# Moving the loads of the cumulative sums to another queue, and one group's stage ahead by a projection, in a hybrid decoder step

## The chip, the cores and the metric

The kernel runs on one core of a Trainium2 chip. The metric is device microseconds of one execution. A core has a matrix engine, TensorE (PE in the profile; PEld is its weight load), three other engines, VectorE (DVE), ScalarE (ACT) and GpSimd (POOL), and SyncE (SP), which here only issues DMAs. Each engine works through its own list of instructions in order and waits on semaphores. [...] The profile writes SPq and ACTq for the issuing of DMAs by SyncE and ScalarE.

## What is computed

Two layers of a hybrid decoder, one step, on a prompt of 256 tokens and on 8 samples of 4 tokens that share the weights: 288 columns in all. Everything is float32.

```python
for l in range(DEPTH):
    x = x + 0.5 * swiglu(rmsnorm(x, norm_ffn1[l]), ...)
    m = mixer(rmsnorm(x, norm_mix[l]), ...)      # gated linear attention and a Mamba-2 branch, merged
    x = x + m
    x = x + 0.5 * swiglu(rmsnorm(x, norm_ffn2[l]), ...)
```

The change lies in the Mamba-2 branch (SSD): 32 heads of 64 channels in 4 groups, 128 state dimensions. For each head, `x` is weighted by `dt`, and with the cumulative sums of the decays and the group's B and C:

```python
acum = cumsum(dt * A)                                        # along the tokens
seg = exp(where(causal, acum[t] - acum[s], -inf))
cb = einsum('nbtgd,nbsgd->nbtsg', Cc, Bc)                    # once per group
y_diag = einsum('nbtsg,nbtsgh,nbsghp->nbtghp', cb, seg, xg)
dS = einsum('nbsgd,nbsgh,nbsghp->nbghpd', Bc, exp(acum[-1] - acum), xg)
y_off = einsum('nbtgd,nbtgh,nbghpd->nbtghp', Cc, exp(acum), h_prev)
```

Outputs are the tokens of both sets and all new states, among them the new SSD states of the prompt (`ssm_p`) and of the samples (`ssm_s`).

## The kernel before

Activations lie with their channels on the partitions, `[128, 288]` a block of 128 channels. A projection makes one such block of output. Its weights come as one DMA of 512 KB into `wr` (`weights`, L179, SyncE's queue, four buffers), ScalarE rounds them into `wh` (L166), VectorE takes the rest into `wl` (L172, three buffers of each), and TensorE adds 24 products in one buffer of `psg` (three): 16 with `wh` (L185, L186) and 8 with `wl` (L188). So each projection needs SyncE, ScalarE, VectorE and TensorE in turn.

In the mixer the Mamba-2 branch is the generator `ssd`. It takes 16 channel blocks j of two heads each; four blocks are a group g. Between its stages it yields a number n, and its caller runs n projections of other parts of the layer there (z, output gates and merge gates), so TensorE has large products beside the small ones. `blocks` makes such projections and hands out their results.

The stages, by line:

- `stage_bc(g)`: projections of the group's B and C, each with its causal convolution (`conv`: ScalarE L874 to L879 copies the projection out of `psg` into `cbuf`, VectorE L881 three times, ScalarE L883, VectorE L885 and L889 give `bcf`).
- `stage_group(g)`: transposes of B into one `pst` buffer; VectorE's L949 reads the last part of it into `bpk`. Products of B and C into a second buffer (L952 to L954), masked into `cb` (L957) and `cbs` (L961). `pst` has four buffers, which all small products share.
- `stage_load(j)`: the samples' states `st`, two DMAs of 256 KB (L989, SyncE; eight buffers). `stage_t(j)`: VectorE transposes them (L998) for TensorE's L1016.
- `stage_x(j)`: the projection and convolution of block j of `x` (`xs`). At its end SyncE issues the load of `acb` (L1031): the cumulative sums of the block's two heads, read from device memory and spread over all 128 partitions, `[128, 512]` words; `acb` has two buffers.
- `stage_m(j)`: ScalarE reads `acb` six times (L1046 to L1048, two heads) into the decay masks `m`, takes their exponential (L1050); VectorE weights `x` (L1054, L1057, L1060, L1063).
- `stage_y(j)`: TensorE's eight products (L1074 to L1081) into one `pst` buffer and the two outer products of the samples' states (L1099), one buffer each; VectorE L1083, L1093 and L1101; ScalarE's copy of the prompt's state into `so` (L1088); the stores of `st` (L1103) and, every second block, of `so` (L1106), all on SyncE.

The loop over j runs `stage_load(j + 3)`, `stage_x(j + 2)`, `stage_m(j + 1)`, yields one projection, then, for j of 2, 6 and 10, runs the next group's `stage_group`, then `stage_y(j)` and further stages.

The order in which the program is written isn't the order on the engines: a scheduler puts each engine's instructions into a list when the program is built. So the change of a few lines moves instructions on all engines, and the order on an engine is shown below as it is built.

## Time and profile before

| | |
|---|---|
| median of 3 runs | 1818.79 us (1818.36 to 1819.49) |
| the profiled execution | 1818.43 us, span 1816.6 us |
| granted clock of TensorE, mean | 0.998 of full speed |
| busy: TensorE / VectorE / ScalarE / GpSimd | 98% / 69% / 57% / 19% |
| bytes moved by DMA | 325.59 MB, 179 GB/s over the span |

Times in the views count from the start of the span. In a timeline the bracket at the end of a line is the time in which the engine stood idle just before the instruction, and what it then waited for last; an x and a number after it join alike instructions in a row. The SSD stage of layer 1 lies at about 369 to 600 us, that of layer 2 at about 1265 to 1500. Since TensorE has 35 us of idle time in all, its own gaps are the place to look, and other engines' waits where such a gap leads to them.

### The profile page before, as it was taken

How to read it: one execution, taken by the hardware profiler on the slowest of the kernel's cores; microseconds unless marked ns; L12 is line 12 of the kernel's file. 1: busy time of each engine (PE TensorE's matmuls, PEld its weight loads, DVE VectorE, ACT ScalarE, POOL GpSimd, SP SyncE). 2: the span in 40 equal slices, each digit the busy share in tenths (PEclk: the TensorE clock that was granted, in tenths of full speed). 3: DMA queues.
4: the chain of work that ended last, by engine and by line, in shares of the span. 5: the costliest groups of instructions: out<-in, count | busy, mean ns of one | idle time of the engine just before them, and what ended most of it. 6: DMA issues, size and time to landing. Idle time of an engine off the chain costs nothing.

```text
span 1816.6 us, 36201 instructions
## 1 busy us (share of the span) xinstructions
PE 1781.6 (98%) x14304; PEld 1722.5 (95%) x14304; DVE 1257.0 (69%) x2091; ACT 1042.3 (57%) x1970; POOL 349.0 (19%) x453
## 2 busy tenths in 40 slices
PE   8999999999999999999999999999998999999997
PEld 8999999889899999999999999998888999999997
DVE  6555578689898767555565556777889987665554
ACT  6444476577677545444454445665877765554443
POOL 1000000055786400000000000000577671000000
PEclk9999999999999999999999999999999999999999
DMA  7655654976878755555555556558778776555553
GB/s 214 172 170 160 164 148 124 276 196 178 216 213 221 197 170 170 167 163 163 170 169 166 166 162 161 147 170 245 195 192 218 210 214 183 170 163 164 169 161 90
DMA packets 613117, 325.59 MB, mean 179 GB/s; under 512 B 17090, under 2 KB 607858, under 8 KB 612948
## 3 DMA queue, kind: packets, MB, share of 16 engines
q1 hardware_dynamic: 612900, 323.15, 63.3%
q8 instruction: 112, 1.84, 0.4%
q14 instruction: 57, 0.47, 0.1%
q10 hardware_dynamic: 48, 0.13, 0.0%
HBM read 293.01 MB, written 30.22 MB: 178 GB/s over the span
## 4 chain that ended last, share of the span: by engine, by line
PE 52%; DVE 3%; ACT 3%; DMA 2%; POOL 1%; issue 1%; DVEq 0%; ACTq 0%; POOLq 0%
PE psg L185 16%; PE psg L188 16%; PE psg L186 16%; DMA wr<-in_w_in_dram 2%; DVE wl L172 1%; POOL st L1005 1%; PE pst L151 1%; ACT wh L166 1%; DVE sT L998 0%; PE pst L1074 0%; PE pst L1099 0%; ACT bm L979 0%; PE pst L810 0%; DVE cacc L881 0%; PE yo L1016 0%
## 5 line engine op out<-in xcount | busy, mean ns | idle before, releaser
L166 ACT ACTIVATE wh<-wr 128x1024 fp32r<-128x1024 f32 (+1 forms) x498 | 518.5, 1042 | 483.2 <-PE psg L186 379.2
L185 PE MATMUL psg<-xh,wh 128*128 128x288 f32 x2704 | 731.9, 298 | 8.9 <-ACT cbuf L875 4.9
L186 PE MATMUL psg<-xl,wh 128*128 128x288 f32 x2704 | 727.7, 296 | 0.1
L172 DVE TENSOR_TENSOR wl<-wr,wh 128x1024 fp32r<-128x1024 f32 (+1 forms) x496 | 595.1, 1201 | 143.4 <-ACT wh L166 141.6
L185 PEld LDWEIGHTS psg<-xh,wh 128*128 128x128 f32 x2704 | 507.4, 188 | 18.6 <-ACT cbuf L875 5.8
L186 PEld LDWEIGHTS psg<-xl,wh 128*128 128x128 f32 x2704 | 507.4, 188 | 3.9 <-issue 0.9
L188 PE MATMUL psg<-xh,wl 128*128 128x288 f32 x2704 | 415.3, 295 | 0.2
L188 PEld LDWEIGHTS psg<-xh,wl 128*128 128x128 f32 x2704 | 375.8, 188 | 2.4 <-issue 0.9
L1005 POOL TENSOR_SCALAR st<-st,decs 128x128 f32<-128x128 f32 x256 | 241.9, 964 | 41.8 <-DVE sT L998 33.9
L185 PE MATMUL psg<-hh,wh 128*128 128x288 f32 x704 | 188.8, 294 | 0.0
L186 PE MATMUL psg<-hl,wh 128*128 128x288 f32 x704 | 188.3, 294 | 0.0
L185 PEld LDWEIGHTS psg<-hh,wh 128*128 128x128 f32 x704 | 132.1, 188 | 0.1
L186 PEld LDWEIGHTS psg<-hl,wh 128*128 128x128 f32 x704 | 132.1, 188 | 0.0
L313 DVE TENSOR_TENSOR t<-t,psg 128x288 f32<-128x288 f32 x88 | 39.9, 454 | 132.8 <-ACT wh L166 119.5
L382 POOL MEMSET cbuf<- 128x3 f32 x4 | 0.3, 108 | 648.2 <-DVE t L333 648.2
L188 PE MATMUL psg<-hh,wl 128*128 128x288 f32 x704 | 108.3, 294 | 0.0
L310 DVE TENSOR_TENSOR t<-psg,rr 128x288 f32<-128x288 f32 x88 | 40.2, 457 | 87.3 <-PE psg L188 87.2
L188 PEld LDWEIGHTS psg<-hh,wl 128*128 128x128 f32 x704 | 98.1, 188 | 0.0
L881 DVE SCALAR_TENSOR_TENSOR cacc<-cbuf,cw,cacc 128x312 f32<-128x312 f32 x144 | 79.0, 548 | 5.4 <-ACT cacc L879 4.9
L185 PE MATMUL psg<-oh,wh 128*128 128x288 f32 x256 | 69.9, 300 | 0.0
L185 PE MATMUL psg<-yh,wh 128*128 128x288 f32 x256 | 69.7, 299 | 0.0
L186 PE MATMUL psg<-ob,wh 128*128 128x288 f32 x256 | 69.1, 295 | 0.0
(317 smaller groups left out, 2234.4 us busy)
## 6 DMA issues: line engine op xcount, KB each, us to landing
wr<-in_w_ffn_gu_dram SPq DMA_DIRECT2D x176, 512.0 KB
wr<-in_w_in_dram SPq DMA_DIRECT2D x160, 512.0 KB
wr<-in_w_ffn_down_dram SPq DMA_DIRECT2D x64, 448.0 KB
wr<-in_w_ffn_down_dram SPq DMA_DIRECT2D x32, 512.0 KB
st<-in_state_ssm_dram SPq DMA_DIRECT2D x64, 256.0 KB
out_dram<-st SPq DMA_DIRECT2D x64, 256.0 KB
wr<-in_w_proj_ssm_dram SPq DMA_DIRECT2D x32, 512.0 KB
gst<-in_state_gla_dram SPq DMA_DIRECT2D x32, 256.0 KB
```

Source lines behind the costliest of these rows:

```text
L151: T.transpose(out, in_, ident[0:k, 0:k])
L166: A.activation(out=h, in_=raw, func=AF.Copy)
L172: V.tensor_tensor(out=lo, in0=raw, in1=h, op=ALU.subtract)
L185: T.matmul(out, lhsT=h[:, k], rhs=xh[k], start=start and k == 0, stop=False)
L186: T.matmul(out, lhsT=h[:, k], rhs=xl[k], start=False, stop=False)
L188: T.matmul(out, lhsT=lo[:, k], rhs=xh[k], start=False, stop=stop and k == n - 1)
L310: V.tensor_tensor(out=t, in0=pg, in1=r, op=ALU.mult)
L313: V.tensor_tensor(out=h, in0=t, in1=pu, op=ALU.mult)
L382: G.memset(cbufs[i][:, 0:3], 0.0)
L881: V.scalar_tensor_tensor(out=acc, in0=buf[:, i:i + NCV], scalar=w[i], in1=acc, op0=ALU.mult, op1=ALU.add)
L1005: G.tensor_scalar(out=st[:, r], in0=st[:, r], scalar1=decs[:, n:n + 1], scalar2=None, op0=ALU.mult)
```

## The change

Three things are edited. The load of `acb` becomes a stage of its own: for blocks 0 and 1 it is issued by SyncE ahead of the first state loads, for block j + 2 by ScalarE in `stage_m(j)`, behind the six reads of the buffer that it fills anew (14 a layer). The store of `so` is issued by ScalarE in place of SyncE (8 a layer). And `stage_group` of the groups 1 to 3 is called ahead of `stage_m(j + 1)` and of the projection behind it, in place of after it. All else is the same; the lines of the functions below the edit have higher numbers in the changed kernel (L1031 becomes L1035, L1046 L1049, L1054 L1059, L1057 L1062, L1060 L1065, L1063 L1068, L1074 L1079, L1076 L1081, L1083 L1088, L1093 L1098, L1099 L1104, L1101 L1106, L1103 L1108).

```diff
@@ -1027,13 +1027,16 @@
                 conv_last(j, buf)
                 x4 = sp_.tile([128, 128], F32, name="b4", tag="b4", bufs=3)
                 pack(A, x4, xs[:, sp])
-                acb = sp_.tile([128, 2, SEQ], F32, name="acb", tag="acb", bufs=2)
-                nc.sync.dma_start(out=acb, in_=acd[2 * j:2 * j + 2].partition_broadcast(128))
-                R["x", j] = xs, x4, acb
+                R["x", j] = xs, x4
+
+            def stage_acb(j, eng):
+
+                R["acb", j] = acb = sp_.tile([128, 2, SEQ], F32, name="acb", tag="acb", bufs=2)
+                eng.dma_start(out=acb, in_=acd[2 * j:2 * j + 2].partition_broadcast(128))
 
             def stage_m(j):
 
-                xs, x4, acb = R.pop(("x", j))
+                (xs, x4), acb = R.pop(("x", j)), R.pop(("acb", j))
                 cb3 = R["g", j // 4][2]
                 p = pst()
                 tr(p[:, 0:128], xs[:, 0:128])
@@ -1046,6 +1049,8 @@
                     A.activation(out=m[:, hh, 0], in_=ab[:, 0:128], func=AF.Relu, scale=-1.0, bias=A0[:, hd:hd + 1])
                     A.activation(out=m[:, hh, 1], in_=ab[:, 128:256], func=AF.Exp, bias=F0[:, hd:hd + 1])
                     A.activation(out=m[:, hh, 2], in_=ab[:, 128:256], func=AF.Relu, scale=-1.0, bias=A1[:, hd:hd + 1])
+                if j + 2 < 16:
+                    stage_acb(j + 2, nc.scalar)
                 m02 = m[:, :, 0:3:2]
                 A.activation(out=m02, in_=m02, func=AF.Exp, scale=-1.0)
                 xg = sp_.tile([128, 3, 128], F32, name="xg", tag="xg", bufs=2)
@@ -1103,10 +1108,12 @@
                     nc.sync.dma_start(out=state_view(ssm_s, j, hf), in_=sts[hf])
                 if j % 2:
                     hg = j // 2
-                    nc.sync.dma_start(out=ssm_p[l, 0, 4 * hg:4 * hg + 4].rearrange("h p d -> (h p) d").rearrange(
+                    nc.scalar.dma_start(out=ssm_p[l, 0, 4 * hg:4 * hg + 4].rearrange("h p d -> (h p) d").rearrange(
                         "(j q) d -> q j d", q=128), in_=so)
 
             stage_bc(0)
+            for j in range(2):
+                stage_acb(j, nc.sync)
             for j in range(3):
                 stage_load(j)
             yield 1
@@ -1132,11 +1139,11 @@
                 if j == 0:
                     stage_bc(1)
                     stage_pack(1)
+                if j in (2, 6, 10):
+                    stage_group(hg // 2 + 1)
                 if j + 1 < 16:
                     stage_m(j + 1)
                 yield 1
-                if j in (2, 6, 10):
-                    stage_group(hg // 2 + 1)
                 stage_y(j)
                 if j + 2 < 16:
                     stage_t(j + 2)
```

SyncE's list at the start of the SSD stage of layer 1, before and then after (a DMA with its destination and source, its shape, and how many in a row):

```order
L179 DMA wr<-in_w_in_dram 128x8x128 x4
L989 DMA st<-in_state_ssm_dram 128x4x128 x6
L1031 DMA acb<-acd 128x512 x2
L989 DMA st<-in_state_ssm_dram 128x4x128 x2
L179 DMA wr<-in_w_in_dram 128x8x128 x2
L1031 DMA acb<-acd 128x512
L179 DMA wr<-in_w_in_dram 128x8x128 x3
L1031 DMA acb<-acd 128x512
L179 DMA wr<-in_w_in_dram 128x8x128 x5
```

```order
L179 DMA wr<-in_w_in_dram 128x8x128 x4
L1035 DMA acb<-acd 128x512 x2
L989 DMA st<-in_state_ssm_dram 128x4x128 x8
L179 DMA wr<-in_w_in_dram 128x8x128 x9
L1108 DMA out_dram<-st 128x4x128 x2
L989 DMA st<-in_state_ssm_dram 128x4x128
L179 DMA wr<-in_w_in_dram 128x8x128
```

The two first broadcasts stand ahead of the state loads, and the later ones no longer stand between the weights.

VectorE's list around block 6 of layer 1, where group 2 is prepared, before and then after (L949, L957 and L961 are the group's; L881 to L889 are a convolution):

```order
L881 SCALAR_TENSOR_TENSOR cacc<-cbuf_2523,cw,cacc 128x312
L1063 SCALAR_TENSOR_TENSOR xpk<-xpk,call,xd 128x128
L172 TENSOR_TENSOR wl<-wr,wh 128x1024
L885 SCALAR_TENSOR_TENSOR xs<-t_6242,cacc 128x256
L889 SCALAR_TENSOR_TENSOR xs<-t_6242,cacc 128x32
L949 SCALAR_TENSOR_TENSOR bpk<-bpk,call,pst 128x128
L957 TENSOR_TENSOR cb_6319<-pst,call 128x2x128
L1083 SCALAR_TENSOR_TENSOR t_6340<-xs,prm,pst 128x288
L1101 TENSOR_TENSOR st<-st,pst 128x512
L961 TENSOR_TENSOR cbs<-pst,call 128x32
```

```order
L949 SCALAR_TENSOR_TENSOR bpk<-bpk,call,pst 128x128
L881 SCALAR_TENSOR_TENSOR cacc<-cbuf_2523,cw,cacc 128x312
L957 TENSOR_TENSOR cb_6266<-pst,call 128x2x128
L881 SCALAR_TENSOR_TENSOR cacc<-cbuf_2523,cw,cacc 128x312
L961 TENSOR_TENSOR cbs<-pst,call 128x32
L1059 TENSOR_TENSOR xg<-pst,dtm 128x384
L885 SCALAR_TENSOR_TENSOR xs<-t_6244,cacc 128x256
L889 SCALAR_TENSOR_TENSOR xs<-t_6244,cacc 128x32
L1062 TENSOR_TENSOR xd<-pst,dec_2515 128x384
L172 TENSOR_TENSOR wl<-wr,wh 128x1024
L1068 SCALAR_TENSOR_TENSOR xpk<-xpk,call,xd 128x128
L1088 SCALAR_TENSOR_TENSOR t_6342<-xs,prm,pst 128x288
```

The group's three instructions move from behind the convolution's last steps to between its first ones, and stand ahead of the same block's L1059 to L1068.

TensorE's list where block 4's `stage_y` meets the projection behind it (layer 1), before and then after (`oh` and `ob` are the parts of the activations of another projection, `xh` and `xl` those of the next):

```order
L186 MATMUL psg<-ob,wh 128x288
L188 MATMUL psg<-oh,wl 128x288 x8
L1074 MATMUL pst<-m,xg 64x256
L185 MATMUL psg<-xh,wh 128x288
L186 MATMUL psg<-xl,wh 128x288
```

```order
L188 MATMUL psg<-oh,wl 128x288 x8
L1081 MATMUL pst<-m,xg 64x128
L1082 MATMUL pst<-mse,xg 128x32
L1083 MATMUL pst<-call,yos 128x32
L1085 MATMUL pst<-bt,xd 128x128
L1086 MATMUL pst<-bt,xd 128x128
L185 MATMUL psg<-xh,wh 128x288
```

Before, one product of `stage_y` stands ahead of that projection's first matmul and the others behind its last; after, all eight stand ahead of it.

## Rows read from the trace of the kernel before

**Rows 1.** The page's first part: engine, busy us, share, instructions.

```profile
PE 1781.6 (98%) x14304; PEld 1722.5 (95%) x14304; DVE 1257.0 (69%) x2091; ACT 1042.3 (57%) x1970; POOL 349.0 (19%) x453
```

**Rows 2.** TensorE's timeline, layer 1: start us, us, what, [idle before <-releaser].

```profile
382.79 0.40 PE L185 MATMUL psg<-xh,wh 128*128 128x288 f32 x1 [1.07 <-DVE yb L488]
...
386.52 0.70 PE L952 MATMUL pst<-bcf 128*128 128x256 f32 x2 [1.50 <-DVE bcf L885]
...
428.48 0.65 PE L1016 MATMUL yo<-sT,cbd 128*32 128x64 f32 x32 [0.87 <-DVE sT L998]
...
468.60 0.40 PE L185 MATMUL psg<-xh,wh 128*128 128x288 f32 x1 [1.97 <-ACT cbuf L875]
...
508.08 0.50 PE L1099 MATMUL pst<-bm,xpk 128*128 128x512 f32 x1 [1.47 <-DVE bpk L949]
```

**Rows 3.** TensorE's timeline, layer 2.

```profile
1279.07 0.40 PE L185 MATMUL psg<-xh,wh 128*128 128x288 f32 x1 [1.51 <-DVE yb L488]
...
1282.32 0.70 PE L952 MATMUL pst<-bcf 128*128 128x256 f32 x2 [1.01 <-DVE bcf L885]
...
1324.27 0.65 PE L1016 MATMUL yo<-sT,cbd 128*32 128x64 f32 x32 [0.78 <-DVE sT L998]
...
1365.25 0.40 PE L185 MATMUL psg<-xh,wh 128*128 128x288 f32 x1 [2.91 <-ACT cbuf L875]
...
1403.26 0.50 PE L1099 MATMUL pst<-bm,xpk 128*128 128x512 f32 x1 [1.54 <-DVE bpk L949]
```

**Rows 4.** Waits of SyncE's queue, 370 to 590 us: total us, times, longest.

```profile
SPq L179 <- DVE wl L172: 74.4, 31, 6.0
SPq L1031 <- ACT m L1048: 21.4, 4, 12.1
```

**Rows 5.** ScalarE's timeline, the rows read.

```profile
379.15 0.40 ACT L1046 ACTIVATE m<-acb,ac 128x128 f32<-128x128 f32 x1 [3.08 <-DMA acb<-acd]
...
383.74 1.06 ACT L166 ACTIVATE wh<-wr 128x1024 fp32r<-128x1024 f32 x1 [0.41 <-DMA wr<-in_w_in_dram]
...
404.97 1.06 ACT L166 ACTIVATE wh<-wr 128x1024 fp32r<-128x1024 f32 x1 [2.81 <-DMA wr<-in_w_in_dram]
...
464.91 1.06 ACT L166 ACTIVATE wh<-wr 128x1024 fp32r<-128x1024 f32 x1 [3.45 <-DMA wr<-in_w_in_dram]
...
1810.70 0.37 ACTq L1245 DMA_DIRECT2D out_dram<-yo  x1
```

**Rows 6.** Stretches: window, us, busy us (instructions) by engine, granted clock, DMA share, GB/s.

```profile
379.00:390.00 11.00, 8.44 (x60) 7.70 (x59) 7.48 (x13) 10.39 (x33) 11.00 (x17) 1.00 1.14 293
394.00:466.00 72.00, 70.84 (x640) 66.68 (x639) 66.21 (x124) 55.05 (x144) 44.02 (x53) 1.00 0.69 186
...
460.00:462.00 2.00, 2.00 (x17) 2.00 (x17) 1.99 (x4) 1.13 (x3) 2.00 (x2) 1.00 0.66 138
...
470.00:472.00 2.00, 2.00 (x11) 2.00 (x10) 2.00 (x4) 0.40 (x3) 0.00 (x0) 0.50 0.51 122
```

The engines stand there in the order PE, PEld, DVE, ACT, POOL.

**Rows 7.** VectorE's timeline, two places.

```profile
427.29 0.52 DVE L1093 SCALAR_TENSOR_TENSOR yb<-yb,prm,yh 128x288 fp32r<-128x288 f32 x1 [0.68 <-ACT yh L1091]
...
507.69 0.33 DVE L949 SCALAR_TENSOR_TENSOR bpk<-bpk,call,pst 128x128 fp32r<-128x128 f32 x1
```

**Rows 8.** SyncE's timeline: issues of DMAs.

```profile
373.44 2.28 SPq L1031 DMA_DIRECT2D acb<-acd  x2
...
376.85 3.26 SPq L179 DMA_DIRECT2D wr<-in_w_in_dram  x2
...
457.98 0.46 SPq L1031 DMA_DIRECT2D acb<-acd  x1
458.91 1.83 SPq L179 DMA_DIRECT2D wr<-in_w_in_dram  x2
```

**Rows 9.** TensorE's timeline, one block's stage_y: first product, first outer product.

```profile
447.61 0.66 PE L1074 MATMUL pst<-m,xg 128*64 128x256 f32 x4
...
449.33 0.72 PE L1099 MATMUL pst<-bm,xpk 128*128 128x512 f32 x2
```

## The prediction, made before the changed kernel ran

> **What bounds the kernel now.** I read the busy shares first: TensorE (PE) is busy 1781.6 us of a span of 1816.6 [rows 1], so everything still to be had is its 35 us of idle time, and every other wait counts only as far as it ends in one of TensorE's gaps. Next comes TensorE's own timeline, for what released it after each gap. In the part that the change touches (state-space stage, about 369 to 600 us in layer 1 and 1265 to 1500 in layer 2) five gaps stand out in each layer. In layer 1 they are 1.07, 1.50, 0.87, 1.97 and 1.47 us [rows 2], in layer 2 1.51, 1.01, 0.78, 2.91 and 1.54 [rows 3]. That is 6.88 and 7.75 us, 14.6 together. A forecast is a statement on these ten gaps, and on new ones.
>
> Then the queues. SyncE (SP) issues in order, so a load that waits for a buffer holds all behind it. Its issue of `acb` (L1031) waits for the last reader of the old `acb`, ScalarE's L1048, four times in layer 1, 21.4 us in all and 12.1 the longest [rows 4]; the next weights stand right behind it in SyncE's order. ScalarE (ACT) then stands 2.81 us for weights at 404.97 [rows 5], and VectorE (DVE) behind it. VectorE is busy 66.2 of the 72 us from 394 to 466 [rows 6] and so has little room to catch up there.
>
> **The change part by part.**
>
> *Group stage one projection earlier.* TensorE's last gap, 1.47 and 1.54 us at L1099 [rows 2, 3], waits for `bpk`: the second outer product needs the fourth `pst` buffer, which still holds the transposes of the next group until VectorE's L949 has read them, and that stands at 507.69 behind the convolution's L885 and L889 [rows 7]. In the new order L949, L957 and L961 are interleaved with L881, a whole projection ahead of L1106 (the old L1101), so the buffer is free long before. The same instructions run on the same engines, and TensorE's transposes and products of the group only change places with weight matmuls. What is late next at that place is VectorE's L1088 (the old L1083), which the eight products of stage_y feed and which TensorE doesn't wait for there. Price: −1.47 −1.54 = **−3.0**. Bounds: −3.0, and 0 if another user of the four buffers is as late.
>
> *First two `acb` ahead of the states.* ScalarE's 3.08 us at L1046 [rows 5] go: these two broadcasts were issued at 373.44 [rows 8] behind six state loads, now ahead of them. But TensorE is in order and needs more than that. Its next gap, at L952, hangs on C's convolution: L885 needs ScalarE's L883, which stands behind an L166 that itself waited 0.41 us for weights at 383.74 [rows 5]. Those weights were issued from 376.85 on [rows 8] behind eight state loads and two broadcasts; the bytes ahead of them are the same in either order, and the DMAs move 293 GB/s in 379 to 390, with a busy share of 1.14 of their engines [rows 6]: there is no room for more. So when `acb` no longer delays ScalarE, the first gap melts into the second and the end of the pair stays where the weights put it. What is new is `acb` 2: ScalarE now issues it as soon as stage_m(0) has read `acb` 0, some 5 us before its place in the old order, and so while those weights are in flight. It has 128x512 words of 4 bytes, 0.262 MB, and 0.262/293 = 0.9 us at the full rate. Price: +0.9 a layer, **+1.8**. The trace of before has no broadcast on ScalarE's queue, so both bounds: −5.1 if both gaps of both layers go (1.07 + 1.50 + 1.51 + 1.01), and +3.8 if it costs its bytes at the 138 GB/s that ran at 460 to 462 [rows 6], shortly after SyncE's broadcast at 457.98 [rows 8]: 1.9 a layer. I take 0.9 because its row is from this very stretch.
>
> *The other 14 broadcasts a layer, and the stores of `so`, off SyncE's queue.* The waits of 12.1 and less [rows 4] go, and with them ScalarE's 2.81 us. On TensorE this can give back no more than the gap that VectorE causes further on in the same stretch: 0.87 us at 428.48, where the states' transposes L998 come late [rows 2], with a 0.68 us wait of VectorE just ahead of them [rows 7]; 0.78 in layer 2 [rows 3]. In the new order two L998 stand ahead of L1098 (the old L1093), so that wait doesn't delay them either. Price: −0.87 −0.78 = **−1.6** (bounds −1.6 and 0).
>
> *Issue time on ScalarE.* 14 + 8 issues a layer at 0.37 us each (the one DMA that ScalarE issues in the trace [rows 5]) are 8.1 us a layer. About six fall in the stretch where VectorE sets the pace: 2.2 us, less than the 2.81 that goes, and ScalarE is busy 55.1 of 72 us there [rows 6]. Behind such an issue L1050 and the next L166 are queued, and VectorE's L172 waits for the latter. I take 0 for it; bounds 0 and +2.2 a layer, if the cover of 2.81 doesn't come about.
>
> *Gap at 468.60 and 1365.25.* The largest, 1.97 and 2.91 us [rows 2, 3]. It ends with ScalarE's L875, which stands behind an L166 that waited 3.45 us for weights at 464.91 [rows 5]. SyncE issued those from 458.91 on, after a broadcast at 457.98 [rows 8]; but they could not go before VectorE's L172 had released their buffer, and that chain is not touched. So the end of the gap stays. What changes is TensorE's order: the eight products of stage_y, which in another block run from 447.61 to 449.33 (1.72 us [rows 9]), stood here all but the first behind the stalled weight matmuls, and now they stand ahead. They fill 1.72 us less some 0.25 for the first, 1.47 a layer: **−2.9**. Bounds: 0 if they are late too, −4.9 if the gap goes altogether. Behind the gap TensorE ran at 0.50 of its clock (470 to 472 [rows 6]), 1.2 GHz instead of 2.4; in layer 1 that could go too, worth up to 1.7 us if 3.4 us at half speed become full ones. I count none of it.
>
> **Sum.** 1818.43 − 3.0 + 1.8 − 1.6 + 0 − 2.9 = 1812.7 for an execution like the profiled one. Its span is 1816.6, with 1.8 around it; the median of the runs is 1818.79, 0.4 above it. Against that median: **1813.0**.
>
> **Rivals.** *(a) Only the group stage counts.* The queue change takes waits away from engines that were not the bound; the weights' landing and VectorE's load stay, the matmuls in the big gap are themselves late, and the start costs 0 to +1.8. 1818.43 − 3.0 + 0 to 1.8 = 1815.4 to 1817.2. For it: TensorE is busy 70.8 of the 72 us in the stretch where SyncE is blocked longest [rows 6]. Against it: the gaps at 428.48 and 468.60 have late VectorE and ScalarE work as releasers [rows 2].
> The Trainium skill, "DMA: Bandwidth & Descriptors", section "Issuing engines are not separate DMA queues", speaks for this rival: DMAs started by scalar, sync or gpsimd run on the same 16 engines, and several issuers save only the sequencer's time. By it the move between queues is worth 0 and only the 3.0 remain, 1815.4; the trace disagrees in that what SyncE loses is in-order waiting, 12.1 us at its longest, and not issue time.
>
> *(b) The weights come early.* SyncE, never held by `acb`, gets its weights out before TensorE is short of them: the big gap and the half clock go as well (1.97 + 2.91 + 1.7 − 2.9 = 3.7 more), 1809; if the first two gaps of each layer also go, another 6.9 (5.1 instead of −1.8), 1802. Against it: SyncE's weight loads wait for VectorE's L172 31 times, 74.4 us in all [rows 4], three times as much as for `acb`, and that stays.
>
> *(c) Slower: broadcasts cut in ahead of weights.* On SyncE's queue a broadcast went out in its turn; on ScalarE's it is in flight beside weights that are awaited. Each time it takes 0.262 MB at 138 GB/s, 1.9 us, from weights that ScalarE waits for. Over the two places of each layer where ScalarE waits long (around 404 and 464 [rows 5]) that is +7.6, less 3.0 of the group stage: 1823.0. It decides if a broadcast is issued within some 5 us ahead of such a wait: 6 us lie between issue and use at 458.91 and 464.91 [rows 5, 8].
>
> *(d) The change doesn't do what it says.* ScalarE's in-order queue holds the broadcast so late that stage_m waits for it: 1818 to 1820. Little speaks for it, since the issue stands right behind the reads that free the buffer, a whole projection ahead of its use.
>
> **How the numbers follow.** Forecast, 1810 to 1815: 0.45. (a) 0.30. (b) 0.09. (c) 0.13. (d) 0.03. A measurement of this kernel can tell about 0.2% from no change, 3.6 us: faster means under 1815.2, slower over 1822.4. The forecast and (b) are faster, with a little of (a): 0.55. Most of (a) and (d) are the same: 0.32. (c) is slower: 0.13. The range takes in the forecast, (a), (d) and the nearer end of (b), down to 1807.5 and up to 1820; the term with the widest bounds, the start (−5.1 to +3.8), lies within it on both sides. Beyond it are (c) and the far end of (b).
>
> **What would show it.** In the profile of the changed kernel: no gap at the second outer product in either layer (group stage); no wait of ScalarE for `acb` at the start, and one gap of 2.5 to 3.4 us before the group's first product (start); no wait of 2.8 us for weights at about 405, and none of TensorE for L998 near 428 (queue); at 468 and 1365 gaps of about 0.5 and 1.4, with the products of stage_y ahead of them. Wrong would be: a new gap released by ScalarE's L166 or by `acb`, more waiting for weights on ScalarE than before, or VectorE as busy in 394 to 466 and TensorE's gaps there unchanged.

## The result, and the profile of the changed kernel

The changed kernel takes 1850.8 us (median of 4 runs, 1846.3 to 1852.3) against 1818.6 of the kernel before: a ratio of 1.017 (95% interval 1.0157 to 1.0183), so it is 32 us slower. Forecast were 1813.0 us, faster, with 1807.5 to 1820 as the range. The profiled execution took 1851.06 us, span 1849.3.

The first part of the page, to be held against [rows 1]:

```profile
PE 1801.1 (97%) x14304; PEld 1737.4 (94%) x14304; DVE 1261.8 (68%) x2091; ACT 1043.1 (56%) x1970; POOL 341.2 (18%) x453
```

TensorE's idle time is 48.2 us instead of 35.0, 13.2 more. But it is also busy 19.5 us longer with the same 14304 instructions: its granted clock is 0.988 on the mean, against 0.998. In the two state-space stages the clock now stands at half for seven stretches, beside or behind gaps, where the kernel before had one; the longest gap, 3.40 us at 390.85, has none behind it. Two windows of the changed kernel (columns as in [rows 6]; 0.50 is 1.2 GHz) lie around the gap of 3.38 us and behind that of 3.25 us in the list further down:

```profile
1297.00:1303.00 6.00, 4.55 (x18) 4.37 (x19) 2.35 (x5) 4.05 (x17) 4.11 (x9) 0.50 0.86 233
1523.00:1529.00 6.00, 6.00 (x27) 5.56 (x24) 6.00 (x13) 3.24 (x11) 6.00 (x9) 0.50 0.87 241
```

TensorE's timeline of the changed kernel, the long gaps of layer 1 and five of layer 2; the first three answer to [rows 2]:

```profile
385.07 0.40 PE L185 MATMUL psg<-xh,wh 128*128 128x288 f32 x1 [1.17 <-DVE yb L488]
390.85 0.48 PE L952 MATMUL pst<-bcf 128*128 128x256 f32 x1 [3.40 <-DVE bcf L885]
474.68 0.40 PE L185 MATMUL psg<-xh,wh 128*128 128x288 f32 x1 [0.51 <-ACT cbuf L875]
480.59 0.40 PE L185 MATMUL psg<-xh,wh 128*128 128x288 f32 x1 [2.02 <-ACT t L568]
513.25 0.47 PE L1104 MATMUL pst<-bm,xpk 128*128 128x512 f32 x1 [0.87 <-DVE cbs L961]
541.02 0.40 PE L185 MATMUL psg<-xh,wh 128*128 128x288 f32 x1 [1.15 <-ACT cbuf L875]
578.66 0.50 PE L1104 MATMUL pst<-bm,xpk 128*128 128x512 f32 x1 [1.70 <-DVE bpk L949]
...
1298.45 0.80 PE L952 MATMUL pst<-bcf 128*128 128x256 f32 x1 [3.38 <-DVE bcf L885]
1371.14 0.33 PE L151 MATMUL pst<-call,xs 128*128 128x128 f32 x1 [1.55 <-DVE xs L885]
1391.83 0.40 PE L185 MATMUL psg<-xh,wh 128*128 128x288 f32 x1 [2.03 <-ACT t L568]
1453.32 0.40 PE L185 MATMUL psg<-xh,wh 128*128 128x288 f32 x1 [1.99 <-ACT cbuf L875]
1520.74 0.53 PE L188 MATMUL psg<-xh,wl 128*128 128x288 f32 x2 [3.25 <-DVE wl L172]
```

There are new gaps late in the stage, at 541, 578, 1453 and 1520, where the kernel before had nothing over 0.6 us. To see where the time goes I took TensorE's matmuls with weights (L185, L186, L188; 11760 in either trace), and at the same matmul the start in one kernel minus the start in the kernel before. How much this difference grows in a stretch of the stage (bounds in us of the kernel before) is what that stretch cost. The bounds stand where the same small products lie ahead of that matmul in every version; within a stretch the versions order them differently, so it can't be split further. The runs of the other rows are told further on; each is one profiled execution, so a us or so is chance.

| growth, us | start (375 to 403; 1268 to 1296) | middle (403 to 544; 1296 to 1433) | last (544 to 630; 1433 to 1521) | elsewhere | sum |
|---|---|---|---|---|---|
| changed kernel, layers 1 and 2 | 2.0, 4.1 | 2.5, 7.5 | 5.3, 7.5 | 3.8 | 32.7 |
| after_again | 3.3, 3.4 | 2.9, 4.4 | 5.7, 6.0 | 1.1 | 26.7 |
| e_group | −0.1, −0.4 | 0.3, −1.4 | −0.7, 0.0 | 0.8 | −1.5 |
| e_queue | 1.4, 2.8 | 1.7, 2.8 | 6.0, 3.8 | 2.8 | 21.2 |
| e_acbq | 1.9, 3.1 | −1.1, 1.7 | 4.8, 0.4 | 0.5 | 11.3 |
| e_first | 1.2, 1.1 | −0.5, −0.3 | −0.7, 0.0 | 4.2 | 5.0 |
| e_small | 1.0, 0.6 | −1.0, −0.8 | 2.6, 2.3 | 0.3 | 5.1 |
| a_acbsp | 1.1, 1.5 | −2.0, 2.2 | 2.2, 2.6 | 0.3 | 7.8 |
| p_behind | 2.7, 2.9 | −1.1, 0.1 | 0.2, 0.6 | 0.4 | 6.0 |
| l_after | 1.5, 1.9 | 5.8, 7.7 | 5.1, 6.0 | 0.3 | 28.2 |
| a_st10 | 3.5, 3.8 | 1.0, 1.0 | 0.7, 1.6 | −0.2 | 11.3 |
| b_st10 | 0.1, −0.1 | 0.1, 1.1 | 1.2, 1.9 | 0.0 | 4.2 |
| g610 | −0.2, 0.3 | −1.9, −1.5 | 1.8, 2.0 | −0.2 | 0.3 |
| g6 | −0.4, 0.0 | −0.8, −1.8 | 1.2, 1.4 | 0.4 | 0.1 |

The 3.8 us elsewhere of the changed kernel include twice 1.5 us at half clock in the attention stage, which the edit doesn't touch; the same kernel profiled again (after_again) shows 1.1 elsewhere, so that is chance.

What stands behind the late gaps is shown by the chain that ended last. Its shares by line over the state-space stage of layer 2 (1262 to 1545 us), first of the kernel before and then of the changed one:

```profile
by line: PE psg L185 14.1%; PE psg L188 14.0%; PE psg L186 13.7%; DMA wr<-in_w_in_dram 10.3%; POOL st L1005 4.5%; DVE wl L172 3.5%; issue 3.1%; ACT wh L166 2.6%; DVE sT L998 2.3%; PE pst L1074 2.2%; PE pst L1099 1.9%; ACT bm L979 1.7%; DVE 
```

```profile
by line: DMA wr<-in_w_in_dram 10.8%; DMA out_dram<-st 10.2%; DVE wl L172 9.4%; PE psg L185 8.0%; PE psg L188 7.8%; PE psg L186 7.6%; DVE cacc L881 6.0%; DMA st<-in_state_ssm_dram 5.4%; issue 5.1%; DVE st L1106 2.0%; ACT wh L166 1.9%; DVE t 
```

TensorE's weight matmuls fall from 42% of the chain to 23%. Stores and loads of the samples' states, not among the chain's leading lines before, make 16%. The chain itself, in order of time (start, us, what), over the last blocks of layer 2 in the changed kernel:

```profile
1477.90 1.21 DVE st L1106 x2
1479.16 6.78 DMA out_dram<-st
1485.95 2.84 DMA st<-in_state_ssm_dram
1488.79 1.18 DVE wl L172
...
1507.95 0.61 POOL yb L1094
1508.56 6.33 DMA out_dram<-st
1514.91 3.07 DMA st<-in_state_ssm_dram
...
1520.74 1.32 PE psg L188 x8
```

An update of a state buffer (L1106), 6.8 us until its store has landed, 2.8 us for the next load into the same buffer, then VectorE's transpose L998 and all that stands behind it on VectorE, a weight split among it. `st` has eight buffers, two a block, so the load of block j + 4 waits for the store of block j. Two rows of waits over the whole execution, of the kernel before and then of the changed one (total us, times, longest), show this loop closing:

```profile
SPq L989 <- DMA out_dram<-st: 43.3, 39, 3.8
DVE sT L998 <- DMA st<-in_state_ssm_dram: 11.6, 6, 3.2
```

```profile
SPq L989 <- DMA out_dram<-st: 91.4, 42, 5.4
DVE sT L998 <- DMA st<-in_state_ssm_dram: 43.1, 11, 6.6
```

What goes out around a store: issues of DMAs at blocks 8 and 9 of layer 1, SyncE's queue of the kernel before, then SyncE's and ScalarE's of the changed one:

```profile
546.02 0.99 SPq L1103 DMA_DIRECT2D out_dram<-st  x2
547.11 0.50 SPq L1031 DMA_DIRECT2D acb<-acd  x1
549.44 0.38 SPq L989 DMA_DIRECT2D st<-in_state_ssm_dram  x1
...
556.97 0.98 SPq L1103 DMA_DIRECT2D out_dram<-st  x2
...
560.98 1.65 SPq L989 DMA_DIRECT2D st<-in_state_ssm_dram  x2
```

```profile
555.31 0.97 SPq L1108 DMA_DIRECT2D out_dram<-st  x2
560.90 1.11 SPq L989 DMA_DIRECT2D st<-in_state_ssm_dram  x2
562.41 3.11 SPq L179 DMA_DIRECT2D wr<-in_w_in_dram  x3
566.19 1.76 SPq L1108 DMA_DIRECT2D out_dram<-st  x2
572.83 1.03 SPq L989 DMA_DIRECT2D st<-in_state_ssm_dram  x2
```

```profile
554.34 0.33 ACTq L1035 DMA_DIRECT2D acb<-acd  x1
565.53 0.33 ACTq L1035 DMA_DIRECT2D acb<-acd  x1
```

Before, the broadcast goes out behind the two stores, and the first load follows 3.4 us after the first store at block 8, 4.0 us at block 9. Now it goes out 0.7 to 1.0 us ahead of them (554.34, 555.31; 565.53, 566.19), and the load follows after 5.6 and 6.6 us. That the place and the bytes of the broadcast are the reason is what the runs below test. SyncE stands in front of that load all the while, so its weight loads come three in a row at 562.41, right ahead of the next stores.

### The profile page after: what moved, and what is told of

The parts are those of the page before. It is cut to its first block, busy times and chain, and to the rows that moved or that the text cites. A ratio compares the mean times of both kernels' runs of the same rounds, so it can differ in the third digit from the quotient of the medians.

```text
span 1849.3 us, 36211 instructions
## 1 busy us (share of the span) xinstructions
PE 1801.1 (97%) x14304; PEld 1737.4 (94%) x14304; DVE 1261.8 (68%) x2091; ACT 1043.1 (56%) x1970; POOL 341.2 (18%) x453
## 2 busy tenths in 40 slices
DMA packets 613117, 325.59 MB, mean 176 GB/s; under 512 B 17090, under 2 KB 607858, under 8 KB 612948
## 4 chain that ended last, share of the span: by engine, by line
PE 49%; DVE 5%; DMA 4%; ACT 1%; issue 1%; POOL 0%; SPq 0%; DVEq 0%; ACTq 0%
PE psg L185 15%; PE psg L188 15%; PE psg L186 15%; DMA wr<-in_w_in_dram 2%; DVE wl L172 2%; DMA out_dram<-st 2%; DVE cacc L881 1%; DMA st<-in_state_ssm_dram 1%; PE pst L151 1%; ACT wh L166 0%; DVE st L1106 0%; DVE t L1088 0%; PE pst L810 0%; DVE sT L998 0%; PE gyo L801 0%
## 5 line engine op out<-in xcount | busy, mean ns | idle before, releaser
L185 PE MATMUL psg<-xh,wh 128*128 128x288 f32 x2704 | 740.6, 300 | 10.3 <-ACT t L568 4.1
L186 PE MATMUL psg<-xl,wh 128*128 128x288 f32 x2704 | 735.4, 298 | 0.1
L185 PEld LDWEIGHTS psg<-xh,wh 128*128 128x128 f32 x2704 | 514.1, 191 | 20.0 <-ACT t L568 4.9
L186 PEld LDWEIGHTS psg<-xl,wh 128*128 128x128 f32 x2704 | 514.2, 190 | 3.6 <-issue 0.9
L188 PE MATMUL psg<-xh,wl 128*128 128x288 f32 x2704 | 417.8, 296 | 6.1 <-DVE wl L172 6.0
L188 PEld LDWEIGHTS psg<-xh,wl 128*128 128x128 f32 x2704 | 378.0, 189 | 11.5 <-DVE wl L172 8.9
L1005 POOL TENSOR_SCALAR st<-st,decs 128x128 f32<-128x128 f32 x256 | 229.4, 913 | 44.7 <-DVE sT L998 44.5
L185 PE MATMUL psg<-hh,wh 128*128 128x288 f32 x704 | 188.8, 294 | 0.0
L186 PE MATMUL psg<-hl,wh 128*128 128x288 f32 x704 | 188.3, 294 | 0.0
L185 PEld LDWEIGHTS psg<-hh,wh 128*128 128x128 f32 x704 | 132.1, 188 | 0.1
L186 PEld LDWEIGHTS psg<-hl,wh 128*128 128x128 f32 x704 | 132.1, 188 | 0.0
L188 PE MATMUL psg<-hh,wl 128*128 128x288 f32 x704 | 108.3, 294 | 0.0
L188 PEld LDWEIGHTS psg<-hh,wl 128*128 128x128 f32 x704 | 98.1, 188 | 0.0
L881 DVE SCALAR_TENSOR_TENSOR cacc<-cbuf,cw,cacc 128x312 f32<-128x312 f32 x144 | 78.4, 544 | 3.2 <-ACT cacc L879 3.0
L998 DVE STREAM_TRANSPOSE sT<-st 128x512 f32<-128x512 f32 x64 | 43.5, 696 | 43.1 <-DMA st<-in_state_ssm_dram 43.1
L185 PE MATMUL psg<-oh,wh 128*128 128x288 f32 x256 | 69.9, 300 | 0.0
L185 PE MATMUL psg<-yh,wh 128*128 128x288 f32 x256 | 69.7, 299 | 0.0
```

Of the source, the lines that this page charges most:

```text
L185: T.matmul(out, lhsT=h[:, k], rhs=xh[k], start=start and k == 0, stop=False)
L186: T.matmul(out, lhsT=h[:, k], rhs=xl[k], start=False, stop=False)
L188: T.matmul(out, lhsT=lo[:, k], rhs=xh[k], start=False, stop=stop and k == n - 1)
L881: V.scalar_tensor_tensor(out=acc, in0=buf[:, i:i + NCV], scalar=w[i], in1=acc, op0=ALU.mult, op1=ALU.add)
L998: V.transpose(out=R["sT", hg][hf][:, j % 2], in_=st.rearrange("p s d -> p (s d)"))
L1005: G.tensor_scalar(out=st[:, r], in0=st[:, r], scalar1=decs[:, n:n + 1], scalar2=None, op0=ALU.mult)
```

## Each edit alone

*The group's stage alone* (e_group): the kernel before with this only.

```diff
+                if j in (2, 6, 10):
+                    stage_group(hg // 2 + 1)
                 if j + 1 < 16:
                     stage_m(j + 1)
                 yield 1
-                if j in (2, 6, 10):
-                    stage_group(hg // 2 + 1)
```

> The kernel before, with the group's stage moved ahead by one projection and nothing else; the broadcasts and the stores of the prompt's state stay on SyncE. Theory A (order): the loss comes from VectorE's state transposes L998, which stand further ahead in VectorE's list once SyncE's list loses the broadcasts and the stores of so; this edit alone moves none of them, so only the two gaps at the outer product go: 1818.6 - 3.0 = 1815.6 us, and VectorE's wait for the state loads stays at about 11.6 us in all. Theory B (contention: ScalarE's ring beside SyncE's delays stores, state loads and weights): the same 1815.6. Theory C (the group's instructions, one projection earlier, push VectorE's other work back): 1825 us or more, and the state waits rise.

Measured: 1817.9 us against 1818.8, ratio 0.9999 (0.9989 to 1.0008). No loss, so theory C falls; but no 3.0 us either. In the profile the gap at block 6 goes in both layers, and the table shows the gain in layer 2 (−1.4) and not in layer 1 (0.3), where it is lost again ahead of block 6: the big gap stays (1.88 us, after 1.97), while in layer 2 it shrinks from 2.91 us and pays for what the edit costs there.

```profile
470.73 0.45 PE L185 MATMUL psg<-xh,wh 128*128 128x288 f32 x1 [1.88 <-ACT cbuf L875]
...
1365.01 0.40 PE L185 MATMUL psg<-xh,wh 128*128 128x288 f32 x1 [1.51 <-ACT cbuf L875]
```

*The queue edits without the group's stage* (e_queue): the changed kernel with the diff above undone.

> The changed kernel with the group's stage back in its old place: only the queue edits (broadcasts and stores of so on ScalarE, the first two broadcasts ahead of the states). Theory A and theory B: the loss stays, 1848 to 1854 us, with VectorE waiting some 40 us for state loads as in the changed kernel (43.1). Theory C: under 1825 us.

Measured: 1835.8 us (1830.2 to 1842.7), ratio 1.0096 (1.0062 to 1.0130); state waits of VectorE 30.2 us. Over half of the loss, but not all, which no theory had: the group's stage, worth nothing alone, costs some 14 us more on top of this (1849.9 in the next section). So the parts don't add up. With the group's stage ahead, VectorE's L998 of block 9 waits 3.9 and 4.3 us for its load, without it 0 and 0.5; that fits a loop through VectorE that is already the pace, but no run shows what the 14 us are made of.

*The stores of `so` alone* (e_so):

```diff
-                    nc.sync.dma_start(out=ssm_p[l, 0, 4 * hg:4 * hg + 4].rearrange("h p d -> (h p) d").rearrange(
+                    nc.scalar.dma_start(out=ssm_p[l, 0, 4 * hg:4 * hg + 4].rearrange("h p d -> (h p) d").rearrange(
```

> The kernel before, with only the stores of the prompt's state (so) issued by ScalarE in place of SyncE. They are 128 KB each, 8 a layer. Theory A (order): in VectorE's list three L998 move ahead by one weight split (blocks 11 and 15), and two of these waited 2.2 to 5.7 us in the changed kernel, so VectorE's state waits rise by 5 to 15 us over both layers and the time to 1822 to 1832 us. Theory B (contention): these small stores cost their bytes at most, 0.13 MB at 293 GB/s = 0.4 us each where they collide: 1818 to 1822 us. Theory C: 1818.6 us.

Measured: 1819.7 against 1818.8, ratio 1.0008 (0.9997 to 1.0019), state waits 12.5 us. Three L998 did move ahead in VectorE's list, and it cost almost nothing: against theory A.

*The broadcasts alone* (e_acbq): the changed kernel with the group's stage and the stores of `so` put back.

> The kernel before, with only the broadcasts changed: first two ahead of the state loads on SyncE, the other 14 a layer on ScalarE behind their last readers; the stores of so stay on SyncE and the group's stage in its old place. Theory A (order): two L998 of block 11 move ahead by one weight split and block 9's does not (it does with the so edit too), so about half of the loss: 1828 to 1840 us. Theory B (contention): the broadcasts on a second ring are the cause, so nearly all of it: 1845 to 1853 us. Theory C: 1815 to 1820 us.

Measured: 1829.9, ratio 1.0061 (1.0041 to 1.0080), state waits 18.9 us. The size is that of theory A, the place isn't: the long waits are at blocks 13 and 15 (up to 5.0 us), whose transposes had not moved in the list. Their loads were issued later: at block 13 of layer 1 7.5 us after the start of the update that frees the buffer, against 4.8 in the kernel before. So neither A nor B fits as it stood.

*The first two broadcasts alone* (e_first):

```diff
+            for j in range(2):
+                stage_acb(j, nc.sync)
             for j in range(3):
                 stage_load(j)
...
-                acb = sp_.tile([128, 2, SEQ], F32, name="acb", tag="acb", bufs=2)
-                nc.sync.dma_start(out=acb, in_=acd[2 * j:2 * j + 2].partition_broadcast(128))
+                if j > 1:
+                    stage_acb(j, nc.sync)
```

> The kernel before, with only the first two broadcasts of each layer issued ahead of the state loads; all others stay on SyncE in their old places, behind each block's convolution. What the start is worth without a broadcast on ScalarE. The changed kernel lost 3.3 us a layer up to the fourth projection of the stage, and 0.8 with the later broadcasts cut to a sixteenth. Theory D: this edit alone costs that 0.6 to 1.0 a layer: 1820 to 1821 us. Theory J (the state loads, two broadcasts later, are the loss at the start): 1824 us or more.

Measured: 1820.5 against 1818.6, ratio 1.0008 (0.9997 to 1.0019); the start grew by 1.2 and 1.1 us. As theory D had it: this edit by itself gains nothing. The time alone doesn't tell the loss from chance; the start shows about 1 us a layer. With no broadcast on ScalarE's queue, ScalarE's wait for weights in layer 1, 0.41 us before [rows 5], is now

```profile
387.26 1.06 ACT L166 ACTIVATE wh<-wr 128x1024 fp32r<-128x1024 f32 x1 [1.75 <-DMA wr<-in_w_in_dram]
```

## The broadcasts: bytes, ring or place

*The changed kernel once more* (after_again), as the mark for the next three.

> The changed kernel itself, beside the next three on the same chip. All theories: 1846 to 1852 us, as when it was first timed; it is the mark for the runs beside it.

Measured: 1849.9 (1845.2 to 1853.7), ratio 1.0159 (1.0135 to 1.0182).

*The same kernel with small broadcasts* (e_small):

```diff
-                R["acb", j] = acb = sp_.tile([128, 2, SEQ], F32, name="acb", tag="acb", bufs=2)
-                eng.dma_start(out=acb, in_=acd[2 * j:2 * j + 2].partition_broadcast(128))
+                acb = R["acb", j] = acbs[j % 2]
+                n = 128 if j < 2 else 8
+                eng.dma_start(out=acb[0:n], in_=acd[2 * j:2 * j + 2].partition_broadcast(n))
```

> The changed kernel, with the broadcasts of blocks 2 to 15 cut to 8 of their 128 partitions, from 256 KB to 16 KB (the other partitions keep the sums of blocks 0 and 1, so the decay masks of the later blocks are not the real ones). Issues, waits and the order on every engine stay as in the changed kernel. Theory D (collision): the broadcast, issued by ScalarE about 1 us ahead of the state stores, lies with its bytes between a store's issue and its landing; the next state load waits for that landing, SyncE with it, and VectorE's L998 for the load. Without the bytes the state waits of VectorE fall from 43 us to 20 or less and the time to 1818 to 1828 us. Theory A (order): L998 stands too far ahead in VectorE's list, bytes or not: 1843 to 1852 us and state waits above 35 us.

Measured: 1823.6, ratio 1.0017 (1.0008 to 1.0027). 26 of the 30 us hang on the bytes of 28 broadcasts, 6.9 MB of 325.59 MB (28 x 240 KB). Order, waits and issue time on ScalarE, all still there, are worth 4 to 5 us together with the rest of the edit. Yet VectorE still waits 29.2 us for states, where theory D had 20 or less: the sum of these waits isn't the price.

*Broadcasts and stores of `so` on SyncE again, the rest as changed* (a_acbsp):

```diff
                 if j + 2 < 16:
-                    stage_acb(j + 2, nc.scalar)
+                    stage_acb(j + 2, nc.sync)
...
-                    nc.scalar.dma_start(out=ssm_p[l, 0, 4 * hg:4 * hg + 4].rearrange("h p d -> (h p) d").rearrange(
+                    nc.sync.dma_start(out=ssm_p[l, 0, 4 * hg:4 * hg + 4].rearrange("h p d -> (h p) d").rearrange(
```

> The changed kernel, with the broadcasts of blocks 2 to 15 and the stores of so issued by SyncE; the first two stay ahead of the state loads and the group's stage stays ahead. In SyncE's list the broadcasts stand behind the state stores again, and L998 stands in VectorE's list as in the kernel before. Theory A and theory D: 1814 to 1821 us, and state waits of VectorE of 10 to 15 us. Theory E (the early start and the group's stage together are the loss, not the queue): 1830 us or more. The two gaps at the start of each stage tell what the first edit is worth alone.

Measured: 1826.0 against 1819.8, ratio 1.0035 (1.0023 to 1.0047); state waits 16.5 us. With all bytes, but behind the stores on SyncE's queue, 24 us of the loss are gone. What is left, 5 us above the expected bound of A and D and 4 below that of E, lies at the start (1.1, 1.5), in the middle of layer 2 (2.2) and in the last stretch (2.2, 2.6).

*The broadcast on ScalarE, but behind the update* (p_behind):

```diff
+                if behind is not None:
+                    V.tensor_copy(out=acb[:, 0, 0:1], in_=behind[:, 0, 0:1])
                 eng.dma_start(out=acb, in_=acd[2 * j:2 * j + 2].partition_broadcast(128))
...
-                if j + 2 < 16:
-                    stage_acb(j + 2, nc.scalar)
+                if j == 0:
+                    stage_acb(2, nc.scalar)
...
                     nc.sync.dma_start(out=state_view(ssm_s, j, hf), in_=sts[hf])
+                if j + 3 < 16:
+                    stage_acb(j + 3, nc.scalar, sts[1])
```

> The changed kernel, with ScalarE's broadcasts (from block 3 on) held until the state update that precedes the stores has run: VectorE copies one column of the updated state into the new buffer right behind that update, which the broadcast then overwrites, so the broadcast is issued at the stores' time or after it, and not a microsecond before them. Ring, bytes and the order of all else stay. Theory K (place: what hurts is that the broadcast is ahead of the stores): 1820 to 1830 us, near the version with all on SyncE (1826.0). Theory L (ring: a broadcast on a second ring shares the DMA engines with the stores wherever it stands, where on SyncE's ring it would wait its turn behind them): 1838 us or more.

Measured: 1831.0 against 1818.6, ratio 1.0065 (1.0046 to 1.0084); runs from 1824.4, which is the profiled one, to 1833.1. A us above the bound of theory K and 7 below that of L. The issues at the same blocks, SyncE's and then ScalarE's:

```profile
546.60 1.93 SPq L1110 DMA_DIRECT2D out_dram<-st  x2
548.91 0.38 SPq L989 DMA_DIRECT2D st<-in_state_ssm_dram  x1
...
559.24 0.97 SPq L1110 DMA_DIRECT2D out_dram<-st  x2
563.66 2.06 SPq L989 DMA_DIRECT2D st<-in_state_ssm_dram  x2
```

```profile
549.72 0.33 ACTq L1037 DMA_DIRECT2D acb<-acd  x1
560.68 0.33 ACTq L1037 DMA_DIRECT2D acb<-acd  x1
```

The broadcast goes out 3.1 and 1.4 us behind the stores, and the load follows after 2.3 and 4.4 us instead of 5.6 and 6.6. In the last stretch of the stage, where the loop of the state buffers sat, the profiled run shows almost no loss (0.2, 0.6), and none in the middle (−1.1, 0.1). So it was the place of the broadcast, up to a us ahead of the stores, that hurt there, as far as this run tells: it is the fastest of the four. By the median some 12 us remain. The profiled run has 6 of them, nearly all at the start (2.7, 2.9), where this edit leaves the broadcast of block 2 as it was. What the slower runs lose besides, and whether the second queue (the ring of theory L) has a part in it, is not settled.

## The loop of the state buffers

*Transposes later* (l_after): the changed kernel with `stage_t(j + 2)`, and `stage_h` behind it, called after the next yield.

> The changed kernel, with the state transposes of block j + 2 and the products that read them moved behind the next yielded projection, so that L998 stands one to four weight splits later in VectorE's list. The queues are as in the changed kernel. Theory A: the state waits fall under 12 us and the time to 1816 to 1825 us. Theory D: the same fall of the waits, but the stores and loads stay late (a load is issued 7 us after the update that frees its buffer, as in the changed kernel), so the weights behind them in SyncE's list stay late too: 1822 to 1838 us. Theory F (the waits for states are only a sign, weights on ScalarE are what is late): 1843 us or more.

Measured: 1846.9, ratio 1.0150 (1.0124 to 1.0175), state waits 12.4 us. The waits fell about as far as theory A said, and next to nothing was won. Theory A is out: VectorE waited less, the load still came late, and all that needs the state came later too. SyncE's waits for stores are still 77.8 us (91.4 in the changed kernel, 43.3 before). The time is that of theory F and not of theory D; what tells against F, that late weights are all of it, is the next run.

*Ten state buffers* (a_st10, and b_st10 on the kernel before):

```diff
-ST_BUFS = 8
+ST_BUFS = 10
...
-            yh = sp_.tile([128, 16, NT], F32R, name="yh")
+            yh = sp_.tile([128, 12, NT], F32R, name="yh")
```

> The changed kernel with ten state buffers in place of eight. The room comes from yh, folded from 16 to 12 blocks: the last four blocks' outputs overwrite the first four, so the tokens are not the reference's; the work on every engine is the same. Theory D' (the loop of the state buffers is the pace: store, its landing, next load, L998, GpSimd's decay, the products, the update, and the broadcast's bytes stretch it): with ten buffers a load waits for a store of one block earlier, so the loop has some 12 us more; VectorE's state waits fall under 12 us and the time to 1820 to 1830 us, what remains being the start of each stage. Theory G (the broadcasts' bytes hurt because weights land late; the state waits only go along): 1840 us or more.

> The kernel before with ten state buffers, and yh folded in the same way: what the two buffers are worth where the loop isn't the pace. Theory D': TensorE sets the pace in the kernel before, so 1815 to 1820 us. Theory G: the same.

Measured: a_st10 1832.7 against 1818.6, ratio 1.0076 (1.0059 to 1.0093), state waits 2.1 us; b_st10 1821.5, ratio 1.0009 (1.0000 to 1.0018). Between the two theories' bounds, nearer to D': 17 of 31 us are gone, and in the table they are gone from the last stretch (5.3 and 7.5 us become 0.7 and 1.6) and from the middle (2.5 and 7.5 become 1.0 and 1.0), while the start costs as much as in the changed kernel. What is left in the last stretch isn't the loop's: the kernel before with ten buffers loses 1.2 and 1.9 us there too, 1.5 us above its expected bound in all, with a gap that the kernel before doesn't have and that belongs to the folded `yh`:

```profile
624.43 0.40 PE L185 MATMUL psg<-yh,wh 128*128 128x288 f32 x1 [0.86 <-ACT yh L1091]
```

So the loss has two parts. The larger one, late, is the loop of the state buffers. The other is the start, 7.3 of the 11.3 us left in this profile (14 by the median), and lies where weights are awaited, as theory G has it.

## Where the group's gain went

*Groups 2 and 3* (g610), and *group 2 alone* (g6), moved ahead in the kernel before; of e_group's diff the condition becomes `j in (6, 10)` and `j == 6`, the other groups stay in their old place.

> The kernel before, with the group's stage moved ahead by one projection for groups 2 and 3 only (blocks 6 and 10); group 1 (block 2) stays in its place. When all three were moved, TensorE gained 1.7 to 1.9 us a layer at block 6 and lost 1.5 us a layer around block 2, where VectorE has no room. Theory H (the loss at block 2 comes from the group's five VectorE and ScalarE steps ahead of that projection's): this keeps the gain and drops the loss: 1818.8 - 2 x 1.8 = 1815.2 us, 1814 to 1816. Theory I (the two are chance): 1817 to 1819 us, as with all three moved.

> The kernel before, with the group's stage moved ahead by one projection for group 2 (block 6) only. In all versions where the state loop isn't the pace this place gained 1.6 to 1.9 us a layer in the profile; the other two places lost up to 1.5 and 2.6. Theory H: 1818.7 - 2 x 1.8 = 1815.1 us, 1814 to 1816.5. Theory I (what is gained there is given back later in the stage): 1817.5 to 1820 us.

Measured: g610 1819.9 against 1818.6, ratio 1.0007 (0.9998 to 1.0017); g6 1817.7 against 1818.6, ratio 0.9998 (0.9988 to 1.0008). Theory H falls; theory I has g6 in its range and misses g610 by a us. Both profiles show the gap at block 6 gone, worth 1.7 and 1.9 us from 493 to 544 and in the same stretch of layer 2, and give 1.2 to 2.0 us back in the last stretch (e_group does not, but keeps no gain in layer 1). In g6 the trace shows what takes it: TensorE comes to block 10's second outer product earlier, and waits there for `bpk`, 1.58 us in layer 1 and 1.18 in layer 2, where the kernel before had no gap. VectorE's L949 is no earlier there than before (570.89 against 569.92), since the L998 ahead of it stands for a state load, 2.83 us, as it did before (2.94). TensorE's row and VectorE's, in g6:

```profile
571.28 0.50 PE L1099 MATMUL pst<-bm,xpk 128*128 128x512 f32 x1 [1.58 <-DVE bpk L949]
```

```profile
566.05 0.71 DVE L998 STREAM_TRANSPOSE sT<-st 128x512 f32<-128x512 f32 x1 [2.83 <-DMA st<-in_state_ssm_dram]
```

In g610, where group 3 is moved too, the gaps behind are 0.87 and 0.56 <-`cbs` at block 10, and 1.26 and 1.16 <-`xd` at the end of the stage. So in these two the gain becomes a wait for VectorE, which a state load already holds there in the kernel before. No version tried is faster than the kernel before.

## The prediction, point by point

The sign was wrong. Most of that is one term, the third: the prediction took the broadcasts off SyncE's queue at −1.6, as waits that go. Alone, that edit with the first two broadcasts costs 11 us (e_acbq), and 26 of the whole change's 30 us hang on the broadcasts' bytes (e_small).

*Group's stage* (−3.0). The gap of 1.47 <-`bpk` at block 6 [rows 2] goes where the edit stands alone. The step that failed is that "TensorE's transposes and products of the group only change places" and that nothing else is late behind them: the time is given back elsewhere in the stage (e_group, g610), in g6 at the same wait one group later. In the changed kernel the gap is 0.87, released by `cbs`, and a new one of 1.70 <-`bpk` stands at block 10; `cbs` frees another of the four buffers, which the prediction's bound of 0 had named.

*Start* (+1.8). The end of the pair of gaps hangs on the weights, as forecast, and the bytes of block 2's broadcast do cost; two steps failed. The first gap didn't melt into the second (1.17 us, after 1.07), and moving the first two broadcasts, put at nothing because "the bytes ahead of them are the same in either order", costs 1.2 and 1.1 us by itself (e_first). ScalarE's wait of 3.08 us at L1046 [rows 5] is 1.14 us, and it waits 3.09 us for weights instead. SyncE's, ScalarE's queue and ScalarE at the start of layer 1:

```profile
371.98 9.22 SPq L989 DMA_DIRECT2D st<-in_state_ssm_dram  x8
381.29 9.56 SPq L179 DMA_DIRECT2D wr<-in_w_in_dram  x5
```

```profile
379.53 0.35 ACTq L1035 DMA_DIRECT2D acb<-acd  x1
```

```profile
388.15 1.06 ACT L166 ACTIVATE wh<-wr 128x1024 fp32r<-128x1024 f32 x1 [3.09 <-DMA wr<-in_w_in_dram]
```

The broadcast goes out 1.8 us ahead of the weights, which come later than before: 381.29 against 376.85 [rows 8], of which 2.2 us are the whole program's shift by then. The two gaps together are 4.57 us instead of 2.57; the stretch cost 2.0 and 4.1 us (that of layer 2 with half clock in it), and 3.3 and 3.4 in the second profile of the same kernel, not 0.9: all four lie above even the forecast's upper bound of 1.9 a layer. With small broadcasts it costs 1.0 and 0.6, so the bytes are over half of it.

*Broadcasts and `so` off SyncE* (−1.6). TensorE's gap for L998 at 428 is gone, as forecast. But ScalarE's wait for weights there isn't: 2.20 us at 407.88 against 2.81 [rows 5]. The step that failed is that SyncE's waits of 12.1 and less "go": the waits for `acb` (21.4 us in layer 1 [rows 4]) were replaced by waits for state stores, 48 us more over the execution, and the loop of the state buffers became the pace. The prediction priced what the freed queue would do, and not what the freed broadcast would run into. Two of its own signs of being wrong came up: VectorE is busy 68.6 of the 72 us from 394 to 466, after 66.2, and ScalarE waits 19.1 us in all for these weights, after 16.8.

*Issue time on ScalarE* (0). Near: an issue took 0.33 to 0.48 us, and e_small, with all of them, loses 4 to 5 us with everything else in it; no run shows the issues alone.

*The largest gap* (−2.9). Forecast 0.5 us, measured 0.51 at 474.68, in place of 1.97. But the next projection's gap grew from

```profile
476.38 0.40 PE L185 MATMUL psg<-xh,wh 128*128 128x288 f32 x1 [0.46 <-ACT t L568]
```

to the 2.02 us at 480.59, with half clock behind it. Together 2.53 us against 2.43: nothing won. In layer 2 the gap of 2.91 us goes altogether, where 1.4 were forecast to stay; the next one is 2.03 us, and a new one of 1.55, released by VectorE's L885, stands ahead of them at 1371.14: 3.58 us against 3.37. What failed is a term put at nothing without a reason, TensorE's next wait: having done the work earlier, it is held one projection on by the same late ScalarE, or by VectorE.

*Rivals.* (c) had the right kind: a broadcast on ScalarE's queue cutting in ahead of bytes that are awaited. It named the weights, gave 1823 and a chance of 0.13. At the start it was the weights; over the execution ScalarE's waits for them grew by 2.3 us only. The bytes that mattered most are the state stores', which the prediction never looked at: 43.3 us of SyncE's waits for them stood in the trace of before, and the eight buffers in the code. Of what the Trainium skill states in "DMA: Bandwidth & Descriptors", section "Issuing engines are not separate DMA queues", one half holds here: that DMAs of all issuers run on the same engines and interleave agrees with e_small, where the bytes alone make 26 us. The other half, that several issuers only save issue time, doesn't: the broadcasts alone, moved, cost 11 us (e_acbq), of which the first two, still on SyncE, make about 2, not clear of chance (e_first).

## What to carry to other kernels

A queue that waits also keeps transfers in order: before a DMA is taken out of it, look up what it stood behind, and which transfer it will now overtake or meet. Find the loops that a buffer closes (store, its landing, next load, first use) and compare their length with the time between two uses; here, in the kernel before, the first L998 of blocks 13 and 15 ran 8.4 to 10.5 us after the start of the update that freed its buffer and already waited up to 3.2 us, so 2 us more between store and load made this loop the pace of the stage. A wait that is removed, and a gap that is filled, count only when the next late event on the same path has been named and priced.

## What was not expected of the hardware

Beside or behind several of TensorE's gaps of 1.5 to 3.4 us the granted clock stood at 0.50 for 3.4 or 6.8 us. In all it stood there for 45.7 us of the changed kernel's span, against 11.0 before; half of the difference, about 17 us, is lost to TensorE where it is busy, so this made most of the 19.5 us that TensorE was busy longer, more than the gaps themselves added (13.2). It isn't one to one: 2.91 us at 1365.25 in the kernel before [rows 3] and 3.40 us at 390.85 in the changed one had no such stretch behind them, and shorter gaps in the attention stage had one in one execution and none in another.
